# A sixth pair of gate columns by seven products, gate sigmoids at the producer, and one more LayerNorm row per half on VectorE

## The chip, the cores and the metric

The kernel runs on one core of a Trainium2 chip. The metric is the device time of one execution in microseconds (us), smaller is better; the median of several runs counts. The engines are PE (TensorE, with its weight loads listed as PEld), DVE (VectorE), ACT (ScalarE), POOL (GpSimd) and SP (SyncE, whose queue issues all the DMAs here).

## What is computed

One layer of a transformer-like trunk on x of 1024 rows and 1024 columns, all in float32:

```python
h = x @ w_in                       # 1024 x 5120: q, k, v of two head groups, gates ga, gb
y_a = chunk_band_attention(qa, ka, va, rel_bias) @ w_proj_a   # 8 softmax heads
y_b = stick_breaking_attention(qb, kb, vb) @ w_proj_b         # 8 heads, sigmoid and running products
gate_a = sigmoid(ga + b_gate[:1024]); gate_b = sigmoid(gb + b_gate[1024:])
mix = (gate_a * y_a + gate_b * y_b) @ w_out
x = layer_norm(alpha * x + mix)                               # LayerNorm 1
x = layer_norm(alpha * x + (silu(x @ wg) * (x @ wu)) @ w_ffn_out)
```

## The kernel before

Every float32 operand is split in a high and a low part (`split`, L110), and a product of two is three matmuls: high by high, high by low, low by high. Two schemes make a 1024-column projection. The plain one (`gate`, L542; `project_plain`, L314) takes 48 matmuls of 128x512 for 128 output columns. The other takes two blocks of 128 columns together as a 2 by 2 block matrix product by seven products in place of eight (`pair_steps`, L181): 7 products of 12 matmuls, 84 for 256 columns, where two plain ones take 96. It needs sums of the weights, which `prep_left`, `prep_right` and `prep_last` (L135 to L164) make on DVE and ACT.

The program runs in stages.

- **First stage** (0 to 348 us): one plain q/k pair, one plain gate (`first_gate`), seven q/k pairs by seven products, the values v (`v_stage`), and then `N_GATE` pairs of gates by seven products (`run_pairs(N_QK, len(work), ...)`). In the version before N_GATE is 5: gates 0 to 9 by seven products and gate 10 plain. Gate i = 2c + br is block c of gate a (br 0) or of gate b (br 1). A gate's columns go to DRAM (`g_dr`) without bias and sigmoid.
- **Attention** (348 to 657 us): eight softmax heads (A) and then eight stick-breaking heads (B). Per block of 128 queries PE makes scores (`sc`), ACT and DVE and POOL turn them into weights (`w`), PE transposes these (`tp`), ACT and DVE split them (`pt`), and PE multiplies by v (`pv`). In between stand filler matmuls from `fill_all` (L741): first the plain gates that are left (11 to 15 before, `gps`, 48 units each), then the projection of y_a with its gate (`yAps`, 192 units in all). Each unit is one matmul of 128x512. With the fillers come their weights' loads and splits (`load_w`, L525), the loads and splits of y_a (`split_y`, L792), the reload of a gate from DRAM with its sigmoid on ACT (`reload_gate`, L799), and a multiplication on DVE (L770).
- **y_b, output projection, LayerNorm 1** (657 to about 830 us): the same for y_b (`yBps`), the product with w_out by seven products (`ops`), and LayerNorm 1 row tile by row tile (`layer_norm`, L936), followed by transposes of the result (`x1ps`, L967).
- **FFN** (up to the end): `sxf`, `szf`, `syf` and `dn`.

How many filler units a head gets is set by FILL: the first number is the units of each A head, the second of each B head. The program adds that much to a goal over the head's steps and draws fillers up to it:

```python
        goal += FILL[hd["br"]] / nhead
        fill_until(0.5 * (last + goal))
```

Before, 8 x 16 + 8 x 38 = 432 units, which is 5 x 48 + 192. A scheduler then lays each engine's instructions in an order of its own; each engine then takes its instructions in that order.

`layer_norm` has two ways to apply the last scale and shift. The slow one, for row tiles 0, 1, 4 and 5, is one ACT pass (L951) and one POOL addition (L952) over 128x1024. The quick one, for 2, 3, 6 and 7, is two DVE instructions of 128x512 (L947).

## Time and profile before

| what | us |
|---|---|
| median of 3 runs | 1431.62 (1430.89 to 1433.25) |
| the profiled execution | 1434.07 |
| its span, first to last instruction | 1432.0 |
| granted clock of TensorE | 0.999 |
| busy PE, PEld | 1401.2, 1157.2 |
| busy DVE, ACT, POOL | 1021.5, 686.0, 309.4 |

The profile is of one execution. 2.1 us of its time lie outside the span; the median of the runs is 2.45 us below it. The end of a matmul in the records is modelled, so that matmuls overlap in them (389 ns is listed for a 128x512 matmul); how fast PE goes is read from the starts.

### The profile page before, as it was taken

Reading aid. Unit: us, or ns where it says so; the run is one execution under the profiler, and the core shown is the slowest. Engines: PE = TensorE matmul, PEld = TensorE weight load, DVE = VectorE, ACT = ScalarE, POOL = GpSimd, SP = SyncE. Lnnn points to the kernel's source line nnn. Section 1 sums busy time; section 2 is a strip of 40 time slices with the busy share of each in tenths; the row PEclk is TensorE's granted clock in tenths of the full one; section 3 lists DMA queues with packets and bytes.
Section 4 is the critical chain, followed back from the end, with each engine's and each line's share of the span. In section 5 each row is a group of like instructions: output and inputs, shape, how many; then the busy total and the mean of one; then the engine's idle time right before and its main releaser. Section 6 shows DMA issues by size and latency. Waiting matters only on the chain.

```text
span 1432.0 us, 18804 instructions
## 1 busy us (share of the span) xinstructions
PE 1401.2 (98%) x6592; PEld 1157.2 (81%) x6592; DVE 1021.5 (71%) x1588; ACT 686.0 (48%) x1196; POOL 309.4 (22%) x338
## 2 busy tenths in 40 slices
PE   8999999999999999999999999999999999999997
PEld 6888888888788787778887878888888888888886
DVE  8866467763878988986869996555556544875896
ACT  6444354544787889774223633333333332444540
POOL 0000000002444769661314021111111110200022
PEclk9999999999999999999999999999999999999999
DMA  7566737878875566747852143322332227853521
GB/s 250 169 179 182 236 89 272 304 265 253 209 211 167 173 182 206 216 161 285 317 214 81 67 160 105 106 96 108 111 105 84 91 97 258 318 193 104 170 81 74
DMA packets 98574, 248.75 MB, mean 174 GB/s; under 512 B 10400, under 2 KB 26784, under 8 KB 98480
## 3 DMA queue, kind: packets, MB, share of 16 engines
q1 hardware_dynamic: 98480, 247.56, 52.5%
q8 instruction: 52, 0.85, 0.2%
q14 instruction: 42, 0.34, 0.1%
HBM read 164.39 MB, written 83.13 MB: 173 GB/s over the span
## 4 chain that ended last, share of the span: by engine, by line
PE 84%; DVE 7%; ACT 3%; DMA 3%; issue 2%; POOL 0%; POOLq 0%; DVEq 0%; SPq 0%; ACTq 0%
PE sxf L178 15%; PE dn L1247 15%; PE sxp L178 9%; PE szf L178 7%; PE v L425 5%; PE ops L1106 5%; PE szp L178 5%; PE syf L178 4%; PE gps L549 3%; PE syp L178 2%; PE tp_b L705 2%; PE yAps L767 1%; DVE kp_b L676 1%; PE tp_a L705 1%; PE yBps L118 1%
## 5 line engine op out<-in xcount | busy, mean ns | idle before, releaser
L1247 PE MATMUL dn<-dr,dl 128*128 128x512 f32 x924 | 209.9, 389 | 0.0
L1247 PEld LDWEIGHTS dn<-dr,dl 128*128 128x128 f32 x924 | 173.4, 188 | 36.4 <-DVE x L1099 0.4
L679 POOL TENSOR_TENSOR w_b<-w_b,kp_b 128x511 f32<-128x511 f32 (+3 forms) x96 | 100.5, 1057 | 44.9 <-DVE kp_b L676 38.6
L676 DVE TENSOR_TENSOR_SCAN kp_b<-kp_b,ident_ps 128x512 f32<-128x512 f32 (+3 forms) x96 | 93.1, 970 | 18.1 <-ACT kp_b L674 14.2
L111 ACT CAST dl<-raw 128x512 fp32r<-128x512 f32 x77 | 47.2, 622 | 84.1 <-PE dn L1247 64.5
L1106 PE MATMUL ops<-wr,wl 128*128 128x512 f32 x336 | 78.8, 392 | 0.0
L943 POOL TENSOR_TENSOR mv<-mv,neghalf 128x1 f32<-128x1 f32 x16 | 26.9, 1682 | 236.3 <-DVE mv L942 236.3
L628 POOL MEMSET bias<- 64x64 f32 x8 | 1.2, 145 | 335.6 <-ACT bias L627 335.6
L1106 PEld LDWEIGHTS ops<-wr,wl 128*128 128x128 f32 x336 | 62.5, 188 | 12.5
L112 DVE TENSOR_TENSOR dl<-raw,dl 128x512 fp32r<-128x512 f32 x77 | 53.6, 703 | 25.9 <-ACT dl L111 25.7
L674 ACT ACTIVATE kp_b<-sc_b 128x512 f32<-128x512 f32 (+3 forms) x96 | 49.4, 514 | 19.7 <-PE sc_b L609 16.6
L1044 POOL TENSOR_TENSOR sb<-h 128x512 f32<-128x512 f32 x10 | 15.9, 1594 | 185.6 <-PE syf L178 135.5
L649 POOL TENSOR_SCALAR w_a<-w_a,st_a 128x640 f32<-128x640 f32 (+2 forms) x64 | 43.4, 684 | 56.7 <-DVE st_a L648 37.9
L178 PE MATMUL szf<-x1S63h,wcf 128*128 128x512 f32 x168 | 55.3, 390 | 0.0
L191 DVE TENSOR_TENSOR gt<-sxf,gt 128x512 f32<-128x512 f32 x21 | 14.4, 687 | 55.1 <-PE sxf L178 55.1
L112 DVE TENSOR_TENSOR pt_b<-tp_b,pt_b 128x512 fp32r<-128x512 f32 (+1 forms) x80 | 48.8, 621 | 6.9 <-ACT pt_b L111 6.7
L705 PE MATMUL tp_b<-ident,w_b 128*128 128x128 f32 x288 | 45.3, 274 | 5.0 <-DVE pt_b L112 3.2
L111 ACT CAST pt_b<-tp_b 128x512 fp32r<-128x512 f32 (+1 forms) x80 | 45.6, 572 | 9.1 <-PE tp_b L705 8.6
L675 ACT ACTIVATE w_b<-sc_b 128x511 f32<-128x511 f32 (+3 forms) x96 | 49.6, 517 | 0.0
L646 ACT ACTIVATE w_a<-w_a,st_a 128x640 f32<-128x640 f32 (+2 forms) x64 | 44.6, 697 | 8.8 <-DVE st_a L641 7.1
L1045 POOL TENSOR_TENSOR sa<-h,h 128x512 f32<-128x512 f32 x10 | 15.8, 1584 | 147.5 <-PE sxf L178 135.8
L112 DVE TENSOR_TENSOR pt_a<-tp_a,pt_a 128x512 fp32r<-128x512 f32 x64 | 41.6, 652 | 6.9 <-ACT pt_a L111 6.4
(1520 smaller groups left out, 4181.3 us busy)
## 6 DMA issues: line engine op xcount, KB each, us to landing
raw<-left_dr SPq DMA_DIRECT2D x77, 256.0 KB, 3.0
wo_dr<-wo SPq DMA_DIRECT2D x28, 512.0 KB, 4.0
wr<-wo_dr SPq DMA_DIRECT2D x28, 512.0 KB, 7.7
wLf<-in_w_ffn_in_dram SPq DMA_DIRECT2D x22, 512.0 KB, 4.4
wRf<-in_w_ffn_in_dram SPq DMA_DIRECT2D x22, 512.0 KB, 4.2
rows<-in_w_ffn_out_dram SPq DMA_DIRECT2D x22, 512.0 KB, 6.5
left_dr<-h SPq DMA_DIRECT2D x33, 256.0 KB, 2.0
v_dr<-vst SPq DMA_DIRECT2D x16, 512.0 KB, 3.0
```

Of the source, the lines that this page charges most:

```text
L111: nc.scalar.copy(dst_h, src)
L112: nc.vector.tensor_tensor(dst_l, src, dst_h.bitcast(F32), ALU.subtract)
L178: mm(acc, lw[:, ks], rx, start=(first and kt == i == 0), stop=(kt == 3 and i == 2), skip_group_check=not first)
L425: mm(banks[mt], xs[lw][:, ms], o[:, rx], start=(fresh and kt == n == 0), stop=(kt == 3 and n == 2), skip_group_check=not fresh)
L646: nc.scalar.activation(s[:, 0:w], s[:, 0:w], AF.Exp, bias=st[:, m:m + 1], scale=-1.0, accum_out=st[:, 2:3])
L674: nc.scalar.activation(kp[:, c0:e], sc[:, 0:n], AF.Sigmoid, scale=-1.0)
L675: nc.scalar.activation(be[:, m0:e], sc[:, m0 - c0:n], AF.Sigmoid)
L676: nc.vector.tensor_tensor_scan(kp[:, c0:e], kp[:, c0:e], ident_ps()[:, 0:n], kp[:, c0 - 1:c0] if c0 else 0.0, ALU.mult, ALU.bypass if c0 e ...
L679: nc.gpsimd.tensor_tensor(be[:, m0:e], be[:, m0:e], kp[:, m0 - 1:e - 1], ALU.mult)
L705: tr(tp[:, j:j + P], wt[qb - q0][:, (kb - qb) * P:(kb - qb + 1) * P], ident)
L1106: mm(acc, lw, rx, start=(fresh and n == m == 0), stop=(n == 3 and m == 2), skip_group_check=not fresh)
L1247: mm(acc, lw, rx, start=(fresh and steps[s][1] == n == 0), stop=(last and n == 2), skip_group_check=not fresh)
```

## The change

- N_GATE goes from 5 to 6. Gates 10 and 11 become a sixth pair by seven products at the end of the first stage, gate 12 is the plain gate early in that stage, and gates 13, 14 and 15 are the fillers that are left.
- FILL goes from (16, 38) to (12, 30): 8 x 12 + 8 x 30 = 336 units, which is 3 x 48 + 192.
- Bias and sigmoid of gates 0 to 12 are applied where the gates are made, before the store to DRAM: on the tile of 128x1024 for the paired gates, and in place of the copy out of PSUM for gate 12. `reload_gate` applies them to gates 13, 14 and 15 alone. The load of the bias moves forward.
- In LayerNorm 1, row tiles 1 and 5 take the quick way.

```diff
-FILL = (16.0, 38.0)
+FILL = (12.0, 30.0)
...
-    N_GATE = 5
+    N_GATE = 6
...
+    dma(bg, b_gate)
...
-        dma(bg, b_gate)
...
+    def gate_sigmoid(dst, src, i):
+        col = (i % 2) * 8 + i // 2
+        nc.scalar.activation(dst, src, AF.Sigmoid, bias=bg[:, col:col + 1])
...
         def out_g(side):
+            gate_sigmoid(tl[side], tl[side], 2 * pair + int(side) - 1)
             dma(g_dr[2 * pair + int(side) - 1], tl[side])
...
-            nc.scalar.copy(gt[:, cs], acc)
+            if i == 2 * N_GATE:
+                gate_sigmoid(gt[:, cs], acc, i)
+            else:
+                nc.scalar.copy(gt[:, cs], acc)
...
         dma(t, g_dr[2 * c + br])
-        col = br * 8 + c
-        nc.scalar.activation(t, t, AF.Sigmoid, bias=bg[:, col:col + 1])
+        if 2 * c + br > 2 * N_GATE:
+            gate_sigmoid(t, t, 2 * c + br)
...
-            layer_norm(acc_t[tt], g1, b1, f"1_{tt}", tt % 4 >= 2)
+            layer_norm(acc_t[tt], g1, b1, f"1_{tt}", tt % 4 >= 1)
```

After line 279 the lines of the changed program are numbered higher, by 1 at first and by 8 from the attention stage on (L646 becomes L654).

ACT's order at the seam between the first stage and attention, before. `c_12` are the two halves of the last gate pair, `wh_g` the high part of a filler gate's weights, `w_a` the first softmax blocks, to which L646 applies Exp:

```order
L208 COPY c_12_2763<-szp_2775 128x512
L366 COPY c_12_2735<-sxp_2722 128x512
L532 CAST wh_g_2944<-wr_g_2943 128x1024
L646 ACTIVATE w_a_0_0_2866,st_a_0_2867<-w_a_0_0_2866,st_a_0_2867 128x640
L646 ACTIVATE w_a_0_1_2879,st_a_1_2880<-w_a_0_1_2879,st_a_1_2880 128x640
```

The same place in the changed program, where `c_13` is the last pair:

```order
L340 ACTIVATE c_13_2906<-c_13_2906,bg 128x1024
L371 COPY c_13_2878<-sxp_2865 128x512
L537 CAST wh_g_3908<-wr_g_3907 128x1024
L340 ACTIVATE c_13_2878<-c_13_2878,bg 128x1024
L654 ACT_TABLE_LOAD
L654 ACTIVATE w_a_0_0_3001,st_a_0_3002<-w_a_0_0_3001,st_a_0_3002 128x640
```

Between the last copy out of PSUM and the first Exp there now stand a sigmoid and a load of ACT's function table, beside the cast that stood there before.

SP's queue at the same place, before. `g_dr` are the stores of the last pair's gates, `kl`, `kh`, `qs` the loads for the second head, `v` that of its values:

```order
L592 DMA kl_2855<-k_dr_85 64x1024 x2
L531 DMA wr_g_2943<-in_w_in_dram 128x1024
L360 DMA g_dr_112<-c_12_2763 128x1024
L360 DMA g_dr_111<-c_12_2735 128x1024
L601 DMA v_3006<-v_dr_93 128x8x128
L592 DMA kh_2852<-k_dr_85 64x1024
L589 DMA qs_2850<-q_dr_77 128x1024
L592 DMA kh_2852<-k_dr_85 64x1024
```

And in the changed program (`wr_y_0` are weights of the y_a projection):

```order
L365 DMA g_dr_114<-c_13_2906 128x1024
L536 DMA wr_y_0_4764<-in_w_proj_dram 128x512 x2
L365 DMA g_dr_113<-c_13_2878 128x1024
L600 DMA kl_2990<-k_dr_85 64x1024 x2
L600 DMA kh_2987<-k_dr_85 64x1024 x2
```

Both parts of the second head's keys now stand behind both gate stores; its queries stand ahead of them.

DVE's order in LayerNorm 1 around row tile 5, before (`mv_5`, `mv_6` are the statistics of row tiles 5 and 6):

```order
L944 SCALAR_TENSOR_TENSOR acc_7164<-acc_7164,mv_5_7772,ln1g 128x1024
L1097 SCALAR_TENSOR_TENSOR acc_7165<-acc_7165,ops_2_7265 128x512
L940 BN_STATS bn_6_7808<-acc_7165 128x6
L940 BN_STATS bn_7_7832<-acc_7166 128x6
L941 BN_AGGR mv_6_7809<-bn_6_7808 128x2
L942 TENSOR_SCALAR mv_6_7809<-mv_6_7809 128x1
```

And in the changed program:

```order
L952 SCALAR_TENSOR_TENSOR acc_7166<-acc_7166,mv_5_7774,ln1g 128x1024
L1105 SCALAR_TENSOR_TENSOR acc_7167<-acc_7167,ops_2_7267 128x512
L955 SCALAR_TENSOR_TENSOR acc_7166<-acc_7166,mv_5_7774,ln1b 128x512 x2
L948 BN_STATS bn_6_7810<-acc_7167 128x6
L1105 SCALAR_TENSOR_TENSOR acc_7168<-acc_7168,ops_3_7268 128x512
L949 BN_AGGR mv_6_7811<-bn_6_7810 128x2
```

The two instructions of the quick way stand right behind row tile 6's first addition. For row tile 1 they stand in the same way behind the addition of row tile 3's columns (`acc<-ops_3`).

Counted on PE between the first scores of one head and of the next, the fillers before are 16 and 4 in the first two heads, 16 in each of the next six, 20 in the head where A passes into B, then 38 each in six heads and 68 in the last with what follows it. In the changed program they are 23 and 0, then 6, 10, 12, 12, 12, 12, then 15, six times 30, and 54.

## The prediction, with the chip not yet run

> **What bounds the kernel now.** I began with the page's sums, then took the chain of work that ended last in order of time, then busy time by stretches cut at the first scores of each head (the timeline of PE gives these times), and last PE's waits.
>
> ```profile
> span 1432.0 us, 18804 instructions
> PE 1401.2 (98%) x6592; PEld 1157.2 (81%) x6592; DVE 1021.5 (71%) x1588; ACT 686.0 (48%) x1196; POOL 309.4 (22%) x338
> ```
>
> ```profile
> 181.74 71.17 PE v L425 x314
> ...
> 342.67 2.72 PE szp L178 x12
> ...
> 348.76 3.12 DMA g_dr<-c
> 352.28 8.20 DMA kh<-k_dr
> ```
>
> ```profile
> core 0: us, PE busy (x) PEld busy (x) DVE busy (x) ACT busy (x) POOL busy (x), PEclk, DMA share, GB/s
> 260.00:340.00 80.00, 80.00 (x354) 66.25 (x353) 49.55 (x69) 34.94 (x53) 0.58 (x4) 1.00 0.76 280
> 348.00:360.60 12.60, 11.17 (x62) 8.49 (x61) 9.24 (x36) 9.66 (x22) 7.62 (x9) 1.00 0.92 242
> 360.60:371.60 11.00, 10.72 (x69) 9.43 (x70) 8.54 (x35) 8.49 (x20) 4.30 (x6) 1.00 0.69 176
> 371.60:387.30 15.70, 15.26 (x96) 13.01 (x94) 12.94 (x41) 13.74 (x31) 8.39 (x16) 1.00 0.80 201
> 387.30:403.30 16.00, 15.46 (x94) 13.03 (x95) 12.75 (x43) 12.78 (x31) 8.22 (x12) 1.00 0.91 241
> 403.30:464.50 61.20, 60.99 (x378) 51.60 (x378) 50.45 (x164) 47.62 (x113) 24.27 (x40) 1.00 0.62 183
> 464.50:483.30 18.80, 17.13 (x100) 13.96 (x99) 17.50 (x28) 17.37 (x41) 13.60 (x21) 1.00 0.45 118
> 483.30:526.00 42.70, 42.70 (x246) 37.00 (x245) 36.78 (x47) 32.71 (x76) 27.96 (x43) 1.00 0.61 184
> 526.00:549.60 23.60, 21.88 (x124) 18.45 (x123) 18.53 (x24) 22.78 (x46) 20.53 (x21) 1.00 0.73 220
> 549.60:617.50 67.90, 65.30 (x368) 55.30 (x367) 61.71 (x80) 55.05 (x118) 50.43 (x69) 1.00 0.65 194
> 617.50:657.10 39.60, 36.96 (x206) 30.61 (x205) 31.81 (x44) 29.72 (x55) 17.95 (x19) 1.00 0.58 196
> 800.00:850.00 50.00, 48.03 (x212) 39.09 (x212) 49.39 (x60) 26.57 (x34) 7.37 (x4) 1.00 0.34 116
> ```
>
> The two matmul rows of the chain give PE's price: 2.72 / 12 = 71.17 / 314 = 0.2267 us for one 128x512 matmul. In 260:340 PE is busy all the time and 354 matmuls took 80 us, 0.226 each: the first stage is PE alone, with DVE at 62% and ACT at 44%. Attention is tighter. In 403:464 (four A heads) and 483:526 (two B heads with gate fillers) PE hardly stops, so there every filler costs its 0.2267 us. But DVE stands at 82% and 86% in these two, at 93% in 464:483, and at 61.71 / 67.90 = 91% in the B heads with y_a fillers, where PE idles 2.6 us. What PE waits for in 345:660 is, with one exception, an ACT, DVE or POOL result:
>
> ```profile
> PE tp_b L705 <- DVE pt_b L112: 3.2, 5, 1.8
> PE sc_b L608 <- ACT w_b L675: 2.2, 3, 1.5
> PE tp_b L705 <- POOL w_b L679: 1.7, 1, 1.7
> PE tp_a L705 <- DVE pt_a L112: 1.3, 2, 0.8
> PE sc_a L608 <- DMA kh<-k_dr: 1.2, 1, 1.2
> ```
>
> **First stage: plus 19.0 us.** The sixth pair adds 84 matmuls at the end of a stretch that is PE alone: 84 x 0.2267 = 19.04. Its splits, sums and loads come at the rate that the five pairs before it have in 260:340, so PE goes on covering them. New there are the sigmoids:
>
> ```profile
> L802 ACT ACTIVATE gA<-gA,bg 128x1024 f32<-128x1024 f32 x8 | 9.6, 1195 | 0.7 <-DVE pt_b L112 0.6 <-issue 0.2
> L770 DVE TENSOR_TENSOR gA<-yAps,gA 128x512 f32<-128x512 f32 x16 | 10.9, 679 | 0.7 <-PE yAps L767 0.5
> ```
>
> Two of 1.195 us for each pair of 19.04 us take ACT from 44% to some 56%; PE hides them, and the most they could cost, if each held PE up, is 12 x 1.2 = 14.3. I take 0, since ACT has more than half of each pair's time free. The bias load is 8 KB in SP's queue, well ahead of its use: 0. The plain gate's two sigmoids bring a function table load on ACT early in the stage; next to it PE has the following pairs' products, so 0, and at most the load's own time below.
>
> **Seam to attention: plus 1.2 us for the first two heads.** ACT's rows at the seam and at the one table load that attention has now:
>
> ```profile
> 348.15 0.59 ACT L366 COPY c<-sxp 128x512 f32<-128x512 f32 x1 [7.57 <-PE sxp L178]
> ...
> 349.80 0.83 ACT L646 ACTIVATE w_a<-w_a,st_a 128x640 f32<-128x640 f32 x1
> ...
> 465.90 1.28 ACT L674 ACT_TABLE_LOAD   x1
> 467.20 0.60 ACT L674 ACTIVATE kp_b<-sc_b 128x512 f32<-128x512 f32 x1
> ```
>
> The first Exp starts 1.65 us after the last copy out of PSUM starts. In the changed order a sigmoid (1.2) and a table load (1.28) come in between: 2.5 us later, with all the first head's weights behind it. The keys of the second head wait for the last gate's store (in the chain 3.12 us, then 8.20 us for `kh`), which the sigmoid puts off by 1.2 us, and SP holds everything behind that store. Against this PE now has 23 fillers in place of 16 before the second head's first scores, 1.6 us more work, and 0 in place of 4 in the second head. Three fillers more in these two heads are 0.7 us; the delay of 2.5 us is mostly covered by the drawn-forward work. I put the two heads at +1.2, between 0 (all covered) and +3.7 (1.2 for the store and 2.5 for Exp, nothing covered).
>
> The Trainium skill, "ScalarE: Activation LUTs", section "What ACT_TABLE_LOAD costs", gives 1.28 us for the load and another 1.38 us of drain, 2.66 for a switch. Here the first sigmoid starts 1.30 us after the load starts, so the drain does not show; with it the seam would cost some 1.4 us more by the page, an estimate.
>
> **Attention: minus 17 us of 21.8.** Ninety-six fillers leave, 96 x 0.2267 = 21.8, if PE stays the bound in every head. How much of it comes depends on DVE, whose work per head stays (scans, splits), so I go by stretch, with the fillers counted from the order, and ask what share of the new time DVE would be busy:
>
> - 371.6:403.3, 16 fillers fewer: 31.7 - 3.6 = 28.1, DVE 25.7 / 28.1 = 91%. Taken: -3.6, since PE also idles 1.0 there now.
> - 403.3:464.5, 16 fewer: 61.2 - 3.6 = 57.6, DVE 88%. Taken: -3.4.
> - 464.5:483.3, 5 fewer (1.1). DVE is at 93% with PE waiting 1.7. Taken: -0.5.
> - 483.3:526.0, 16 fewer (3.6); y_a's work starts earlier now, so one L770 of 0.68 comes in. DVE 37.5 of 39.1 would be 96%. Taken: 40.4, -2.3.
> - 526.0:549.6, 8 fewer (1.8). ACT is at 22.78 of 23.60 now; two sigmoids of 1.2 leave it, and about 2.5 L770 of 0.68 come to DVE, 20.2. At 94% that is 21.4: -2.2.
> - 549.6:617.5, 24 fewer (5.4), so two L770 fewer: DVE 60.3. PE alone would give 62.5, DVE at 96.5%. At 94%, 64.2: -3.7.
> - 617.5:657.1, 14 fewer (3.2): 36.4, DVE 85%. Taken: -2.7.
>
> Together with the first two heads: 1.2 - 3.6 - 3.4 - 0.5 - 2.3 - 2.2 - 3.7 - 2.7 = -17.2. The 94% is my choice: 93% is the most that a stretch of attention shows (464:483), 99% is shown in 800:850, where DVE's own chain is the bound and does not pass through three other engines for each block. Were the sigmoids that leave ACT (eight for a, of which one stays) the cause of PE's waits, the walls would fall below PE's price less the present idle time; that is the better end. At y_b another six sigmoids of 1.2 us leave ACT; PE idles only some tenths there, so -0.3.
>
> **LayerNorm 1: minus 0.3 us.**
>
> ```profile
> 753.58 0.69 DVE L1099 TENSOR_TENSOR acc<-ops,acc 128x512 f32<-128x512 f32 x1 [1.34 <-PE ops L1106]
> 757.60 1.41 DVE L947 SCALAR_TENSOR_TENSOR acc<-acc,mv,ln1b 128x512 f32<-128x512 f32 x2
> 778.78 1.27 DVE L944 SCALAR_TENSOR_TENSOR acc<-acc,mv,ln1g 128x1024 f32<-128x1024 f32 x1
> 782.19 2.96 DVE L944 SCALAR_TENSOR_TENSOR acc<-acc,mv,ln1g 128x1024 f32<-128x1024 f32 x1
> ```
>
> ```profile
> 781.72 2.35 POOL L952 TENSOR_TENSOR acc<-acc,ln1b 128x1024 f32<-128x1024 f32 x1 [1.26 <-ACT acc L951]
> ```
>
> ```profile
> PE sxf L178 <- DVE gt L191: 2.0, 2, 1.7
> PE x1ps L967 <- POOL acc L952: 1.8, 1, 1.8
> ```
>
> The quick way costs DVE 1.41 us a row tile. For tile 1 the two instructions fall into the 1.34 us in which DVE waits for PE: 0.1. For tile 5 they come ahead of tile 6's statistics, but the POOL addition goes, and with it the stretch of tile 6's L944, which took 2.96 beside that addition and 1.27 without: 1.41 - 1.69 = -0.3. PE's wait of 1.8 us for that addition goes too, but DVE is 99% busy in 800:850 and PE waits for it there again (2.0 us), so what PE gains at 784 it waits at 847. Hence -0.3, between -1.8 (the wait gained whole) and +1.4 (one tile's instructions wholly late).
>
> **Sum.** 19.04 - 17.2 - 0.3 - 0.3 = +1.2 us on the profiled 1434.07, 1435.3. The median of the runs is 2.45 below that execution, so 1432.8 is what I predict for the median, no change within 0.2% (2.9 us), which is about what a measurement of this kernel can tell.
>
> **Rivals.**
>
> *Faster: PE stays the bound.* For it: 403:464 and 483:526 are PE's alone, and ACT loses 8.4 us of sigmoids in attention, so that waits such as the 1.7 in 526:549 may vanish. Then attention gives 21.8 and 1.7 more, less 1.2 at the seam: -22.3. With 19.04 and LayerNorm's and y_b's -0.6 that is -3.9: 1427.8. Against it: DVE would have to be 96% busy over 68 us, and the one A-to-B stretch at 93% has PE waiting. Chance 0.28.
>
> *Slower: DVE's queue takes PE's place in B.* From 483 on every B head but the first carries y_a fillers in the change, so the stretch that is 91% DVE grows from three heads to some four and a half. If DVE cannot go above that 91%, the walls are 37.5 / 0.91 = 41.2, 20.2 / 0.91 = 22.2 and 60.3 / 0.91 = 66.3: -1.5, -1.4 and -1.6 in place of -8.2. The sum rises by 3.7, and by a further 1 if 617:657 keeps its share: +5.9, 1437.5. The point from which it decides is DVE's share in 549:617: at 93% the result is still within 0.2%, at 91% it is slower. Chance 0.22.
>
> *Slower: the seam.* Nothing covered, +3.7 in place of 1.2, gives 1435.3 on top of the forecast's other terms. Chance 0.07.
>
> *The fillers were free.* If PE has room in attention, removing them saves nothing there and the change costs 19 - 0.6: 1450. Busy PE is no proof against it, since the ends of matmuls are modelled; the evidence is that the starts follow each other at the 0.2267 of the first stage and that 483:526 shows no idle. Chance 0.03.
>
> **How the numbers follow.** The forecast itself, within 2.9 us of 1431.62, has 0.40. Faster by over 0.2% is the first rival, with a little of the forecast's lower edge: 0.29 and 0.39 left for no change. Slower is the three others: 0.32. The range for 8 in 10 goes from 1427.2, the first rival with half a microsecond more, to 1438.6, the DVE rival with 1.1 more for part of the seam.
>
> **What would show it.** In the changed profile the last gate pair should end 19.0 us later, at 367; the first `w_a` Exp some 4 us after that; the B heads with y_a fillers should show DVE at 93 to 95%; L944 of tile 6 should take 1.3; attention should last about 292 us from the first scores to the first `yBps` in place of 309. The prediction is wrong if attention lasts under 288 (PE was the bound) or over 296 (DVE was), or if PE waits in the first stage.

## The result, and the profile after

The changed kernel takes 1440.80 us (median of six runs, 1439.77 to 1442.36) where the kernel before, on the same chip, takes 1432.09 (median of five runs, 1430.89 to 1433.64; a sixth was in a slow state, at 1973.62, and is left out). The ratio is 1.0060 with a 95% interval of 1.0046 to 1.0074: slower by some 8.6 us, more than the 0.2% that a measurement can tell, and above the upper end of the predicted range. The profiled execution took 1442.36.

The page's first lines of the changed kernel:

```profile
span 1440.6 us, 18799 instructions
PE 1404.1 (97%) x6580; PEld 1157.6 (80%) x6580; DVE 1033.1 (72%) x1603; ACT 688.0 (48%) x1197; POOL 303.1 (21%) x334
```

Twelve matmuls fewer, yet PE's busy time grew by 2.9 us: some of its matmuls were slower. Where the 8.6 us of span come from is read by stage, cut at the first scores (348.0 before, 368.6 after), the first `yBps` (657.1, 668.0), the first `ops` (701.7, 712.8) and the first `sxf` (798.4, 806.8):

| stage | before | after | difference | predicted |
|---|---|---|---|---|
| up to the first scores | 348.0 | 368.6 | +20.6 | +19.0 |
| attention | 309.1 | 299.4 | -9.7 | -17.2 |
| y_b | 44.6 | 44.8 | +0.2 | -0.3 |
| output projection and LayerNorm 1 | 96.7 | 94.0 | -2.7 | -0.3 |
| FFN and the rest | 633.6 | 633.8 | +0.2 | 0 |

Attention is the stage that failed. Its stretches in the changed kernel, cut at the first scores of a head as in the prediction (heads are counted from 0; 0 to 7 are A, 8 to 15 are B); the rows from 518.60 on are heads 10, 11, 12, then 13 with 14, and 15:

```profile
core 0: us, PE busy (x) PEld busy (x) DVE busy (x) ACT busy (x) POOL busy (x), PEclk, DMA share, GB/s
368.60:392.00 23.40, 23.04 (x134) 18.49 (x132) 17.38 (x68) 20.12 (x43) 10.90 (x15) 1.00 0.73 202
392.00:419.40 27.40, 27.17 (x172) 23.27 (x173) 24.74 (x85) 23.80 (x59) 12.64 (x23) 1.00 0.70 196
419.40:479.80 60.40, 58.40 (x362) 48.84 (x361) 51.11 (x166) 45.79 (x109) 24.21 (x40) 1.00 0.66 189
479.80:498.10 18.30, 16.16 (x95) 12.81 (x94) 17.01 (x26) 16.95 (x41) 12.91 (x23) 1.00 0.53 146
498.10:518.60 20.50, 19.84 (x116) 16.98 (x115) 18.54 (x25) 17.42 (x40) 14.54 (x22) 1.00 0.75 230
518.60:541.40 22.80, 20.01 (x115) 16.81 (x114) 20.26 (x26) 19.90 (x43) 22.80 (x25) 1.00 0.66 186
541.40:565.60 24.20, 21.43 (x116) 18.25 (x115) 21.61 (x24) 15.52 (x34) 16.30 (x23) 0.93 0.59 196
565.60:591.70 26.10, 21.56 (x115) 18.09 (x114) 21.78 (x28) 17.34 (x40) 16.67 (x24) 0.93 0.48 141
591.70:632.10 40.40, 39.85 (x230) 33.82 (x230) 38.69 (x52) 32.95 (x75) 27.03 (x42) 1.00 0.63 196
632.10:668.00 35.90, 33.85 (x191) 27.79 (x190) 31.08 (x42) 26.61 (x52) 15.79 (x19) 1.00 0.53 183
```

Heads 9, 13 and 14 take 20.1 to 20.5 us each; heads 10, 11 and 12, with the same work on PE, take 22.8, 24.2 and 26.1, together 12 us more. DVE is not their bound: it is at 96% in 591.7:632.1, where PE hardly stops, and below 90% in the three slow heads, where its busy time even holds waits for POOL, as shown below. Two things stand out. POOL is busy for the whole of 518.6:541.4. And the granted clock is 0.93 over 541.4:591.7, 1.00 in every other row.

PE's waits in attention (line numbers are 8 higher than before):

```profile
PE tp_b L713 <- DVE pt_b L112: 11.5, 8, 2.8
PE sc_b L616 <- ACT w_b L683: 2.2, 2, 1.8
PE tp_a L713 <- DVE pt_a L112: 1.7, 3, 0.8
```

The wait for `pt_b` was 3.2 before. Four waits make most of the two sums, by the timeline of PE (the wait stands in brackets, it ends at the row's start):

```profile
526.47 0.66 PE L713 MATMUL tp_b<-ident,w_b 128*128 128x128 f32 x4 [2.79 <-DVE pt_b L112]
549.29 1.11 PE L713 MATMUL tp_b<-ident,w_b 128*128 128x128 f32 x4 [2.77 <-DVE pt_b L112]
567.98 0.50 PE L616 MATMUL sc_b<-kh,qs 128*128 128x512 f32 x1 [1.77 <-ACT w_b L683]
575.48 0.66 PE L713 MATMUL tp_b<-ident,w_b 128*128 128x128 f32 x4 [2.77 <-DVE pt_b L112]
```

Each of the three on DVE lies at the start of a head. There DVE adds the two halves of the last head's values (`yt`, L741, 64x1024, both operands in SBUF; 1.22 to 1.32 us in eleven of the fourteen), then does two scans, then the subtractions for which PE waits. DVE before the first of these waits:

```profile
520.75 2.57 DVE L741 TENSOR_TENSOR yt<-yt 64x1024 f32<-64x1024 f32 x1
523.24 2.59 DVE L684 TENSOR_TENSOR_SCAN kp_b<-kp_b,ident_ps 128x512 f32<-128x512 f32 x2
525.75 1.26 DVE L112 TENSOR_TENSOR pt_b<-tp_b,pt_b 128x512 fp32r<-128x512 f32 x2
```

and POOL at the same time, where `yl` is a filler's subtraction (`split_y`):

```profile
519.84 2.39 POOL L805 TENSOR_TENSOR yl<-yraw,yh 128x1024 fp32r<-128x1024 f32 x1
522.20 1.44 POOL L687 TENSOR_TENSOR w_b<-w_b,kp_b 128x127 f32<-128x127 f32 x1
523.60 2.35 POOL L805 TENSOR_TENSOR yl<-yraw,yh 128x1024 fp32r<-128x1024 f32 x1
```

The addition takes 2.57 us in place of 1.22. POOL's subtraction ends at 522.23, the addition at 523.32, 1.09 later: it does nearly its whole work after POOL's instruction. POOL's next one, a 128x127 multiplication that takes 0.46 elsewhere, takes 1.44 and ends 0.32 after the addition: now POOL waited. At the start of head 11 DVE loses three times running (the second POOL row below holds two multiplications):

```profile
542.03 3.98 DVE L741 TENSOR_TENSOR yt<-yv_b 64x1024 f32<-64x1024 f32 x1
```

```profile
541.43 2.40 POOL L538 TENSOR_TENSOR wl_y<-wr_y,wh_y 128x1024 fp32r<-128x1024 f32 x1
543.78 1.15 POOL L687 TENSOR_TENSOR w_b<-w_b,kp_b 128x255 f32<-128x255 f32 x2
```

Again it ends 1.08 us after the last of the POOL instructions, 544.93. The wait of 1.77 on ACT has another path to the same engine: ACT's cast of a filler weight waits in ACT's queue for a POOL subtraction to free its buffer, and the sigmoids of `w_b` stand behind it:

```profile
566.54 1.04 ACT L537 CAST wh_y<-wr_y 128x1024 fp32r<-128x1024 f32 x1 [2.22 <-POOL yl L805]
```

After two of the three waits of 2.8 us the granted clock fell to one half. Three microseconds after each of them, in order 549.29, 575.48 and 526.47:

```profile
549.50:552.50 3.00, 3.00 (x10) 2.42 (x10) 2.89 (x4) 0.59 (x1) 1.67 (x3) 0.50 0.43 157
...
576.80:579.80 3.00, 3.00 (x11) 2.41 (x10) 2.50 (x4) 0.59 (x1) 2.36 (x4) 0.50 0.73 202
...
526.50:529.50 3.00, 3.00 (x18) 2.56 (x19) 2.89 (x4) 1.18 (x2) 3.00 (x3) 1.00 1.01 229
```

Ten and eleven matmuls start where eighteen did. A clock of 0.93 over 24.2 and 26.1 us is 1.7 and 1.8 us lost, 3.5 in all.

At the other two ends: PE's new wait in the first stage, with ACT's rows beside it,

```profile
PE sxp L178 <- ACT gate L340: 1.1, 1, 1.1
```

```profile
45.37 1.28 ACT L340 ACT_TABLE_LOAD   x1
46.67 0.69 ACT L340 ACTIVATE gate<-gps,bg 128x512 f32<-128x512 f32 x1
```

and its waits from 700 to 1222, where the 1.8 us on POOL in LayerNorm 1 went and did not come back at `sxf`:

```profile
PE sxf L178 <- DVE gt L191: 1.8, 2, 1.4
PE x1ps L975 <- DVE acc L955: 0.2, 1, 0.2
```

### The profile page after: what moved, and what is told of

Its sections match the earlier page's. It is cut to its first block, busy times and chain, and to the rows that moved or that the text cites. A ratio compares the mean times of both kernels' runs of the same rounds, so it can differ in the third digit from the quotient of the medians.

```text
span 1440.6 us, 18799 instructions
## 1 busy us (share of the span) xinstructions
PE 1404.1 (97%) x6580; PEld 1157.6 (80%) x6580; DVE 1033.1 (72%) x1603; ACT 688.0 (48%) x1197; POOL 303.1 (21%) x334
## 4 chain that ended last, share of the span: by engine, by line
PE 85%; DVE 8%; ACT 2%; issue 2%; DMA 1%; POOL 1%; SPq 0%; POOLq 0%; DVEq 0%; ACTq 0%
PE sxf L178 15%; PE dn L1255 15%; PE sxp L178 10%; PE szf L178 8%; PE v L430 5%; PE ops L1114 5%; PE szp L178 5%; PE syf L178 4%; PE yAps L775 2%; PE syp L178 2%; PE tp_b L713 2%; PE tp_a L713 1%; PE gps L554 1%; DVE kp_b L684 1%; PE sc_a L616 1%
## 5 line engine op out<-in xcount | busy, mean ns | idle before, releaser
L1114 PEld LDWEIGHTS ops<-wr,wl 128*128 128x128 f32 x336 | 62.5, 188 | 12.5
L112 DVE TENSOR_TENSOR dl<-raw,dl 128x512 fp32r<-128x512 f32 x77 | 53.5, 701 | 24.2 <-ACT dl L111 24.1
L1052 POOL TENSOR_TENSOR sb<-h 128x512 f32<-128x512 f32 x10 | 20.3, 2027 | 184.4 <-PE syf L178 134.1
L713 PE MATMUL tp_b<-ident,w_b 128*128 128x128 f32 x288 | 46.5, 280 | 11.6 <-DVE pt_b L112 11.5
L713 PEld LDWEIGHTS tp_b<-ident,w_b 128*128 128x128 f32 x288 | 35.5, 143 | 22.1 <-DVE pt_b L112 14.0
L654 ACT ACTIVATE w_a<-w_a,st_a 128x640 f32<-128x640 f32 (+2 forms) x64 | 44.5, 696 | 4.9 <-DVE st_a L649 4.0
```

The lines of the kernel that those rows point to most:

```text
L112: nc.vector.tensor_tensor(dst_l, src, dst_h.bitcast(F32), ALU.subtract)
L654: nc.scalar.activation(s[:, 0:w], s[:, 0:w], AF.Exp, bias=st[:, m:m + 1], scale=-1.0, accum_out=st[:, 2:3])
L713: tr(tp[:, j:j + P], wt[qb - q0][:, (kb - qb) * P:(kb - qb + 1) * P], ident)
L1114: mm(acc, lw, rx, start=(fresh and n == m == 0), stop=(n == 3 and m == 2), skip_group_check=not fresh)
```

## The experiments

Eighteen kernels, in five groups; each group shares one chip and the runs of the kernel before on it. "Ratio" is the time against these, with its 95% interval.

| run | median, us | before there | ratio |
|---|---|---|---|
| the change | 1440.80 | 1432.09 | 1.0060 (1.0046 to 1.0074) |
| ln_only | 1430.57 | 1434.17 | 0.9979 (0.9970 to 0.9989) |
| sig_only | 1438.97 | 1434.17 | 1.0033 (1.0022 to 1.0045) |
| pair_only | 1439.62 | 1434.17 | 1.0033 (1.0020 to 1.0047) |
| add_by_half | 1445.82 | 1434.17 | 1.0083 (1.0068 to 1.0098) |
| split_dve | 1437.20 | 1433.61 | 1.0032 (1.0020 to 1.0043) |
| dma_splits | 1431.03 | 1433.61 | 0.9979 (0.9970 to 0.9987) |
| plain_copy | 1440.63 | 1433.61 | 1.0046 (1.0032 to 1.0061) |
| ln_split_dve | 1434.64 | 1433.61 | 1.0008 (0.9999 to 1.0016) |
| pool_single | 1432.44 | 1433.47 | 0.9991 (0.9982 to 1.0000) |
| ln_dma | 1430.67 | 1433.47 | 0.9982 (0.9973 to 0.9991) |
| mixed | 1438.98 | 1433.47 | 1.0037 (1.0024 to 1.0050) |
| pair_ln_mixed | 1435.61 | 1433.47 | 1.0013 (1.0004 to 1.0021) |
| pieces4 | 1443.44 | 1433.93 | 1.0067 (1.0055 to 1.0079) |
| pieces2 | 1440.68 | 1433.93 | 1.0048 (1.0036 to 1.0060) |
| ln_pieces4 | 1434.76 | 1433.93 | 1.0005 (0.9997 to 1.0014) |
| pair_ln_pieces4 | 1439.74 | 1433.93 | 1.0038 (1.0025 to 1.0051) |
| free_y4 | 1433.48 | 1434.68 | 0.9994 (0.9985 to 1.0002) |
| free_late | 1433.04 | 1434.68 | 0.9986 (0.9976 to 0.9995) |

**The three parts alone.** On the kernel before, LayerNorm 1 only:

```diff
-            layer_norm(acc_t[tt], g1, b1, f"1_{tt}", tt % 4 >= 2)
+            layer_norm(acc_t[tt], g1, b1, f"1_{tt}", tt % 4 >= 1)
```

> Before with the LayerNorm edit alone (row tiles 1 and 5 the quick way). The prediction's term was -0.3 us, because VectorE was taken to hand back what PE gains. The changed profile reads otherwise: from the first output-projection matmul to the first dn matmul it takes 510.0 us against 512.2. If the edit is the whole of that, this kernel is 2 us faster than before; if the prediction's term holds, no difference can be measured.

the sigmoids only (N_GATE 5 and FILL as before),

```diff
+            gate_sigmoid(tl[side], tl[side], 2 * pair + int(side) - 1)
             dma(g_dr[2 * pair + int(side) - 1], tl[side])
...
+            if i == 2 * N_GATE:
+                gate_sigmoid(gt[:, cs], acc, i)
...
+        if 2 * c + br > 2 * N_GATE:
+            gate_sigmoid(t, t, 2 * c + br)
```

> Before with bias and sigmoid at the producers alone (five gate pairs, fillers 16 and 38, LayerNorm as before). Theory A, the sigmoids leave ACT where it is full (526:549) and cost little elsewhere: 2 us faster or so, since the 1.7 us wait there goes and some tenths at y_b. Theory B, the two table loads and the sigmoid in front of Exp take it back: the 1.1 us wait of PE for the plain gate's sigmoid appears at about 47 us, the seam costs one more us, and the sum is within 1 us of before or slower.

and the sixth pair only, the sigmoids where they were:

```diff
-FILL = (16.0, 38.0)
+FILL = (12.0, 30.0)
...
-    N_GATE = 5
+    N_GATE = 6
```

> Before with the sixth pair and fillers 12 and 30 alone (sigmoid at the reload, LayerNorm as before). If the loss of the whole change (8.7 us) comes from the fillers taken out of attention, this kernel is slower than before by 8.7 plus the 2 us that LayerNorm gave, less the 1.3 us of the table load at the start: some 9 us, 1441. If moving the sigmoids is what hurts, it is slower by less than 5.

LayerNorm 1 gains 0.21% (3.0 us); the other two cost 0.33% (4.7 us) each. The parts add up to 0.45%, the whole is 0.60%, within the intervals. In sig_only theory B had the sign, and its 1.1 us wait at the start came; but 3.6 us of the loss lie in the B heads (196.2 us in place of 192.6), which neither theory had. pair_only, slower by 4.7 us by the ratio and 5.5 by the medians, stands at the border of its two cases and decides nothing between them. Both parts that cost do it in the same way. In pair_only the additions at the starts of heads 10, 11 and 12 take 2.57, 1.99 and 3.03 us, and PE waits 2.79, 1.64 and 3.02 there. In sig_only head 12 takes 28.0 us in place of 22.6, PE's longest wait of attention is 4.04 us at 560.85, and ahead of it stands this addition:

```profile
552.79 4.43 DVE L741 TENSOR_TENSOR yt<-yt 64x1024 f32<-64x1024 f32 x1
```

```profile
551.64 1.73 POOL L687 TENSOR_TENSOR w_b<-w_b,kp_b 128x383 f32<-128x383 f32 x2
553.31 2.41 POOL L538 TENSOR_TENSOR wl_y<-wr_y,wh_y 128x1024 fp32r<-128x1024 f32 x1
555.67 0.47 POOL L687 TENSOR_TENSOR w_b<-w_b,kp_b 128x127 f32<-128x127 f32 x1
```

With the sigmoids moved, the scheduler laid this weight's subtraction two places further up in POOL's order, ahead of the 128x127 multiplication and the one behind it, so that the addition met it. The addition ends at 557.22, 1.08 after POOL's last.

**The addition in halves.** After the change, every head's addition in two instructions of 64x512, as the last head has it:

```diff
-                    if hd["i"] == 7:
+                    if True:
```

> The changed kernel with the addition of the value halves (64x1024, both operands in SBUF, which took 2.6 to 4.0 us on VectorE beside a POOL split at three head starts, where PE then waits 2.8 us) made in two parts of 64x512, one behind each half of the head, as the last pair of heads has it already. VectorE's sum of work stays. Theory A, the loss in B is that one long instruction in front of the scans at the head's start: the three waits of 2.8 us fall by half or more, 4 to 6 us faster than the changed kernel, so 3 to 5 us slower than before. Theory B, VectorE's share of the time is the bound: no difference from the changed kernel, 8.7 us slower than before.

Slower still, 1.0083. The waits for `pt_b` got shorter (2.24 at most), but others on ACT's `w_b` of 2.1 and 2.5 us came, and head 10 had POOL at 100% over 24.8 us. Neither theory had that. A half takes 0.69 us alone, and three of them took 2.11, 2.04 and 1.65 beside POOL: now each of two additions per head can be held. That the length of this one addition is the cause fell with it.

**Where POOL's subtractions go.** The subtractions of the fillers' y tiles and projection weights, 11 in all, from POOL to VectorE (the four places like this; the two of the plain gates' weights stay on POOL):

```diff
-                        split_y((28, 34, 40, 46).index(n), nc.gpsimd)
+                        split_y((28, 34, 40, 46).index(n), nc.vector)
```

> The whole change, with the subtractions that belong to the fillers in attention (the plain gates' and the projections' weights, and the y tiles: some 13 of 128x1024, 2.4 us each on GpSimd) on VectorE. Theory 'GpSimd is full and slows VectorE': PE's waits in heads 8 to 12 of attention, 12.9 us in the changed kernel against 5.1 in the kernel before, fall to about 6, the added 13 x 1.24 us of VectorE lie beside PE's work, and the time is 1433 to 1436. Rival 'VectorE's share of time is the limit, as predicted': 16 us more on VectorE lengthen attention by 5 to 10 us, to 1446 to 1451.

all 13 subtractions of the fillers taken away; a DMA copies the high part into the low part's place, so the kernel leaves the low parts out, and PE's work is the same:

```diff
-        lo_eng.tensor_tensor(lo, r, hi.bitcast(F32), ALU.subtract)
+        if lo_eng is nc.gpsimd:
+            dma(lo.bitcast(F32), hi.bitcast(F32))
...
-        eng.tensor_tensor(yl[i], raw, yh[i].bitcast(F32), ALU.subtract)
+        dma(yl[i].bitcast(F32), yh[i].bitcast(F32))
```

> The whole change, with those same subtractions left out and the second operand filled by a copy that a DMA makes of the first, so that it costs neither GpSimd nor VectorE anything (the low parts of these operands are left out of the arithmetic; PE's work is the same). Theory 'GpSimd is full and slows VectorE': the value addition of VectorE takes 1.4 to 1.9 us at the start of each head instead of up to 4, GpSimd stays under 80% in head 10, PE's waits in heads 8 to 12 fall from 12.9 to under 6 us and the time to 1431 to 1435. Rival 'VectorE's own chain at the start of a head, too long for the fewer fillers': the waits stay over 10 us and the time within 2 us of 1440.8.

the plain gate's sigmoid back at its reload:

```diff
-            if i == 2 * N_GATE:
-                gate_sigmoid(gt[:, cs], acc, i)
-            else:
-                nc.scalar.copy(gt[:, cs], acc)
+            nc.scalar.copy(gt[:, cs], acc)
...
-        if 2 * c + br > 2 * N_GATE:
+        if 2 * c + br >= 2 * N_GATE:
```

> The whole change, but the one plain gate at the start of the program is copied as before and takes its sigmoid where it is read again. Theory 'the table load in front of that sigmoid is paid in full': first scores 1.2 to 1.6 us earlier, 1439.3 to 1439.8, with the waits of attention as they are. Rival 'that load is hidden, or comes back at the next sigmoid': 1440.8 plus or minus 0.4.

and the kernel before with LayerNorm 1 as changed and the subtractions on VectorE:

> The kernel before, with the part of the change in LayerNorm 1 alone (1430.6 when run by itself) and the fillers' subtractions on VectorE. Theory 'GpSimd is full and slows VectorE': PE's waits in heads 8, 11 and 13 of attention (1.7, 1.7 and 1.8 us) shrink too and the time is 1427 to 1429.5. Rival 'VectorE's share is the limit': 1434 to 1438.

dma_splits is the run that decides: 1431.03, 9.8 us under the changed kernel by the medians (on two chips; by the ratios, each against the kernel before on its own chip, 0.81%, some 11.6 us). Heads 10, 11 and 12 there:

```profile
517.40:539.30 21.90, 20.16 (x115) 16.97 (x114) 19.32 (x25) 18.93 (x42) 12.61 (x21) 1.00 0.82 244
539.30:559.40 20.10, 20.01 (x115) 16.92 (x115) 19.13 (x26) 16.41 (x37) 12.48 (x21) 1.00 0.81 259
559.40:579.70 20.30, 19.79 (x115) 16.98 (x115) 19.64 (x27) 17.35 (x38) 12.48 (x21) 1.00 0.87 266
```

```profile
PE tp_b L716 <- DVE pt_b L112: 4.2, 8, 0.8
```

Heads 11 and 12 are at the 20 us of their neighbours (22.8, 24.2 and 26.1 became 21.9, 20.1 and 20.3; 1.2 us of the first is a wait for the copy itself), every addition of these heads takes 1.22, the clock is 1.00. The order is not the cause: in these three heads PE's 341 matmuls and DVE's 76 instructions of the changed kernel stand in the same order in dma_splits, ACT's nearly so (110 of 115), and POOL's are the same but for the seven subtractions and one multiplication at the edge. DVE stands at 95% and 97% in the last two rows with PE idle for 0.1 and 0.5 us, so DVE's share is not what bounded these heads. VectorE instead of POOL (split_dve) gets only 3.6 us back: head 10 then is VectorE's,

```profile
516.80:540.50 23.70, 20.57 (x116) 16.77 (x115) 23.56 (x29) 20.27 (x44) 15.96 (x20) 1.00 0.62 179
```

99% busy over 23.7 us. Neither theory's number came there (1433 to 1436, or 1446 to 1451): both engines have too little room in that one head. In ln_split_dve, on the longer heads of the kernel before, the move costs: 1434.64 (ratio 1.0008), in the rival's range, against 1430.57 (0.9979) for LayerNorm 1 alone on another chip.

In plain_copy the first scores start at 366.4 in place of 368.6, but 1.0 of these 2.2 us is there before the sigmoid can play a part: the plain gate's first matmul starts at 30.85 in place of 31.88 (32.83 in ln_only, so this start varies by itself). Counted from it, the first scores come after 335.5 us in place of 336.7: the table load and the sigmoid at the plain gate cost 1.2 us at that point. The 1440.63 lies in the rival's range. The time of the whole is lower by 0.14% by the ratios, but the intervals overlap, and the profiled execution was 2.3 us longer between the first `sxf` and the first `dn`, where nothing was changed (418.3 us there, 416.0 in the changed kernel); whether it pays in the end stays open.

**What in the subtractions does it.** Two one-input operations of POOL in place of each subtraction, nearly as long together, each half as long (the low parts are left out here too):

```diff
+            for _ in range(2):
+                lo_eng.tensor_scalar(lo, hi.bitcast(F32), 1.0, 0.0, ALU.mult, ALU.add)
```

> The whole change, with each of the fillers' subtractions on GpSimd replaced by two one-input operations of GpSimd on the same tile (each some 1.1 us by the 0.684 us of a 128x640 one, so that GpSimd is taken for nearly as long as by one subtraction of 2.4; the low parts are left out of the arithmetic, PE's work is the same). Theory 'sharing': a two-input operation of GpSimd slows VectorE's two-input operations beside it. Then VectorE's value addition takes 1.4 to 1.9 us at the head starts, not up to 4.0, PE's waits in heads 8 to 12 fall from 12.9 to under 8 us, and the time to 1433 to 1436, though GpSimd stays near full in head 10. Rival 'queue': the subtractions stand in front of the w_b multiplications in GpSimd's queue and hold them. Then the waits stay over 10 us and the time is 1438.5 to 1441.

the kernel before with LayerNorm 1 as changed and the DMA's copies (again without the low parts), for the price of the pair without the subtractions:

> The kernel before with LayerNorm 1 as changed, and the fillers' subtractions replaced by a DMA's copy as in the whole change at 1431.0 (low parts left out; PE's work the same as in the kernel before). It says whether the sixth pair with its sigmoids pays once GpSimd's subtractions cost nothing. Theory 'the trade is even at best, +20 us before attention and at most -20 in it': 1427 to 1430 here, so the pair still costs 1 to 4 us. Rival 'only the subtractions stood against the pair': 1431 or more here, so the pair would be level or gain.

the subtractions divided between the engines,

```diff
-                        split_y((28, 34, 40, 46).index(n), nc.gpsimd)
+                        split_y((28, 34, 40, 46).index(n), (nc.vector, nc.gpsimd)[n % 4 // 2])
...
-            nxt = load_proj(0, cc + 1, "op", nc.gpsimd) if cc < 3 else None
+            nxt = load_proj(0, cc + 1, "op", nc.vector) if cc < 3 else None
```

> The whole change, with the first and third of the four y subtractions and those of the projections' later weights on VectorE, the rest on GpSimd. Theory 'GpSimd and VectorE both stand near full in heads 10 to 12, so that the best is a division': 1434 to 1436.5, under the 1437.2 of all on VectorE and the 1440.8 of all on GpSimd, with the granted clock of attention's second half back at 1.00. Rival 'any two-input work of GpSimd beside the head starts costs as much as it saves': 1437 to 1440.

and this without the sigmoids at the producers (the two edits of mixed on pair_only with LayerNorm 1 as changed):

> As the one before, but without the sigmoids at the producers: the sixth pair, LayerNorm 1, and the subtractions divided between VectorE and GpSimd. Theory 'the sigmoids at the producers cost 1.2 to 1.4 us at the start (a table load and a sigmoid in front of the first products) and return nothing, since ScalarE is no bound in attention': 1 to 3 us under the one before, 1431.5 to 1434.5. Rival 'ScalarE's sigmoids at the reload cost about as much in attention': the same within 1 us.

pool_single takes 1432.44: 8.4 of the 9.8 us are back, a little more than 'sharing' had said, though POOL does nearly as much in head 10:

```profile
517.50:539.10 21.60, 20.04 (x115) 16.81 (x115) 19.03 (x26) 19.95 (x43) 21.41 (x29) 1.00 0.64 180
```

But its traces correct the theory as I had put it. A one-input operation of POOL holds the addition too:

```profile
561.38 1.64 DVE L745 TENSOR_TENSOR yt<-yt 64x1024 f32<-64x1024 f32 x1
```

```profile
560.87 1.07 POOL L540 TENSOR_SCALAR wl_y<-wh_y 128x1024 fp32r<-128x1024 f32 x1
561.90 1.43 POOL L691 TENSOR_TENSOR w_b<-w_b,kp_b 128x127 f32<-128x127 f32 x1
```

561.94, the end of POOL's, plus 1.08 is again the addition's end. It is not slowed, it waits for its turn, and a shorter instruction makes that turn shorter. ln_dma and dma_splits are level (0.9982 and 0.9979): without these subtractions the sixth pair with its sigmoids costs and gains the same. The 1430.67 lies between the ranges of its theory and its rival. ln_dma is level with ln_only too (0.9979), so in the kernel before the same subtractions cost nothing that shows. That holds with a reserve, since the copies brought ln_dma new waits on `w_b`, and a stretch at 0.57 of the clock in head 13. Dividing helps less than hoped, mixed is at 1438.98 (1437.20 with all on VectorE), within its rival's range. pair_ln_mixed, without the sigmoids at the producers, is 3.4 us under mixed, and over its range; by the two traces 1.2 of that is there at the first scores (367.6 against 368.8), 0.6 comes in the A heads and 1.8 in the B heads.

**Shorter instructions.** Each subtraction of POOL in four, and in two, with the same arithmetic:

```diff
-        eng.tensor_tensor(yl[i], raw, yh[i].bitcast(F32), ALU.subtract)
+        for c in range(0, 1024, 256):
+            cs = slice(c, c + 256)
+            eng.tensor_tensor(yl[i][:, cs], raw[:, cs], yh[i][:, cs].bitcast(F32), ALU.subtract)
```

> The whole change, with each of the fillers' subtractions on GpSimd cut into four instructions of 256 columns (some 0.65 us each; the arithmetic is the same). Theory 'VectorE's addition waits until the GpSimd instruction under way ends': the additions at the head starts take 1.3 to 2.3 us in place of 2.6 to 4.0, PE's waits in heads 8 to 12 fall from 12.9 to some 7 us, no half clock, 1433 to 1436. Rival 'two inputs on GpSimd slow the addition whatever their length, or GpSimd's fullness holds w_b': additions over 2.5 us still, 1439 to 1442.

> As the one before with two instructions of 512 columns (some 1.25 us each). Theory 'waits out the instruction under way': additions of 1.3 to 2.9 us, between the two: 1434 to 1438, and at or over the one in four pieces. Rival 'two inputs or fullness': 1439 to 1442.

> The kernel before with LayerNorm 1 as changed (1430.6 by itself) and the subtractions in four pieces. Theory 'waits out the instruction under way': the two additions that took 1.88 and 2.51 us there take 1.3 to 1.9, and the time is 1429 to 1430.6; since taking the subtractions away altogether gave 1430.7 there, no more than that can come. Rival 'the pieces' own overhead counts': 1431 to 1433.

> Sixth pair and LayerNorm 1 without the sigmoids at the producers, the subtractions in four pieces. Theory 'the sixth pair is level once the subtractions don't hold VectorE': 1430 to 1433. Rival 'GpSimd is full in head 10 all the same and holds w_b': 1434 to 1438.

All four missed the theory's numbers: 1443.44 (over its rival's too) and 1440.68, no better than the change; the two others 1434.76 and 1439.74, over their rivals' too. Of the additions of pieces4, two of three did get short, 1.32 and 1.61 us in place of 2.57 and 2.56, and each still ends 1.08 after a POOL instruction. In pieces2 they took 1.60 and 1.47, but the third, at the start of head 11, took 4.16: it waited out four POOL instructions in a row, so shorter ones need not mean a shorter wait. But the pieces take longer together (4 x 0.779 = 3.1 us for one of 2.39), and head 10 paid for it:

```profile
L810 POOL TENSOR_TENSOR yl<-yraw,yh 128x256 fp32r<-128x256 f32 x28 | 20.8, 779 | 0.4 <-ACT yh L807 0.4
```

```profile
519.30:545.80 26.50, 21.93 (x115) 18.18 (x114) 19.12 (x26) 20.07 (x43) 26.50 (x41) 0.94 0.56 162
```

Its wall is POOL's busy time (POOL's own waits for DVE count as busy), 26.5 us; POOL was full over the whole head at 22.8 in the changed kernel and 23.6 in pieces2 too. In the changed kernel PE's one long wait in that head is the 2.79 us for DVE. In pieces4 and pieces2 it waited there for POOL's own `w_b` as well, for the first and the second time below:

```profile
PE tp_b L716 <- POOL w_b L690: 2.3, 1, 2.3
PE tp_b L716 <- POOL w_b L690: 1.6, 1, 1.6
```

So two things of POOL's cost time: whole instructions that DVE must wait out, and a head that is full of POOL's work. Cutting trades the one for the other.

**Which subtractions.** The four y subtractions that fall into head 10 replaced by a DMA's copy, the others on POOL (`if i < 4` in `split_y`), and the other way round (the projections' weights and the later y tiles replaced); what is replaced leaves out its low parts:

> The whole change, with only the four y subtractions that fall into head 10 replaced by a DMA's copy (their low parts left out). Theory 'head 10 is GpSimd's': its wall falls from 22.8 to about 21 us with GpSimd at some 70%, heads 11 and 12 keep their waits, and 1 to 3 us come back: 1438 to 1440. Rival 'the full queue of head 10 is what puts the later subtractions beside the head starts': heads 11 and 12 fall too, 1431 to 1435.

> The whole change, with the other group replaced by a DMA's copy: the projections' weights and the later y tiles; the four y subtractions of head 10 stay. Theory 'heads 11 and 12 lose by single held instructions': head 10 stays at 22 to 23 us, heads 11 and 12 fall from 24.2 and 26.1 to 20 to 21, no half clock, and 6 to 9 us come back: 1432 to 1435. Rival 'what head 10 piles up is carried into heads 11 and 12': less than 4 us, 1437 or more.

1433.48 and 1433.04: either group gives 7 to 8 us of the 9.8 back, so their prices don't add. Without the four, head 10 falls from 22.8 to 20.5 us, and heads 11 and 12 fall with it, to 21.1 and 21.4: what 'rival' had said of that run. Without the others, head 10 stays (24.3 us, a half clock in it) and heads 11 and 12 fall to 20.1 and 20.6: what 'theory' had said of that one. So the long waits of heads 11 and 12 seem to need both: the delay that head 10 hands on, and a long subtraction in the way. In free_y4 a subtraction still holds the addition at the start of head 11, for 2.22 us, and PE waits only 1.09 there. How the delay is handed on was not followed through the traces.

No kernel with the sixth pair that computes the whole reference beats the kernel before. Of the kernels that compute it, only ln_only does, at 0.9979.

## Why the prediction was wrong, step by step

**The step that failed** is "attention: minus 17 us of 21.8", in its B heads, and in it the question that was put to each stretch: "what share of the new time DVE would be busy". The stretches of the prediction, with what they gained in the changed kernel and in dma_splits:

| heads | predicted | the change | subtractions by DMA |
|---|---|---|---|
| 0, 1 | +1.2 | -0.2 | -1.0 |
| 2, 3 | -3.6 | -4.3 | -3.4 |
| 4 to 7 | -3.4 | -0.8 | -1.6 |
| 8 | -0.5 | -0.5 | -0.5 |
| 9, 10 | -2.3 | +0.6 | -0.3 |
| 11 | -2.2 | +0.6 | -3.5 |
| 12 to 14 | -3.7 | -1.4 | -6.8 |
| 15 | -2.7 | -3.7 | -3.7 |
| sum | -17.2 | -9.7 | -20.8 |

The 94% of DVE bounded nothing: in heads 11 and 12 of dma_splits DVE is at 95 and 97% with PE idle for 0.1 and 0.5 us. What lengthened heads 10 to 12 was POOL's subtractions: they take 73.1 us with them and 62.3 without. The forecast counted fillers as matmuls only and put their subtractions at nothing, without a reason. Their price comes in two ways. The larger part is that DVE's additions wait out whole POOL instructions and PE waits behind them: pool_single, with POOL still busy for 21.41 of 21.6 us in head 10 but in shorter instructions, got 8.4 us back. The other part is a full POOL, and the row for it stood in the prediction, unread: POOL was busy 20.53 of 23.60 us in 526:549.6, with four y subtractions, and in the change these fall into head 10, for which the forecast had some 20.2 us (half of 40.4). Their place counts too: before, the first of them started 5.6 us behind the start of its head and none met an addition; in the change the first starts at 516.77, 1.8 us ahead of the start of head 10, and the next one holds the addition there. A head that gets shorter keeps POOL's work, 12.5 us of `w_b` (dma_splits shows it alone), and in this one head four y subtractions of 2.39 and one weight of 2.42 on top.

**The DVE rival** (1437.5) had the right sign and place, B heads from 483 on, but its mechanism is refuted by the same rows. **PE stays the bound** (1427.8) is nearly what dma_splits shows in attention, -20.8 against -22.3, once POOL's subtractions are gone. That the fillers were free is refuted: attention got 9.7 us shorter even so. The seam was no loss: the first Exp starts 4.1 us after the first scores in place of 1.9, much as forecast, and heads 0 and 1 still gained 0.2.

**The A heads** came out right in sum (-5.3 for -5.8) by luck, since the parts were wrong: in heads 4 to 7 sixteen fillers fewer gave 0.8 us and not 3.4, in dma_splits 1.6, so a filler there was worth 0.05 to 0.1 us and not 0.2267. Busy PE without recorded waits was no proof that each of its matmuls has its full price: 60.99 of 61.2 us were busy before, and 58.40 of 60.40 after.

**First stage**: 84 x 0.2267 was the right size, and 0 was right for the pairs' sigmoids: from the plain gate's first matmul to the first scores plain_copy, which has them, takes 19.0 us more than the kernel before (335.5 and 316.5). "The plain gate's two sigmoids ... 0, and at most the load's own time" was not: PE waited 1.1 us there, the first scores came 1.6 us later than forecast, and 1.2 us, counted from the plain gate, went with the sigmoid in plain_copy. The cover I named, the products behind it, was not there, since PE's next product needs a bank that the plain gate holds until its sigmoid has read it; that last reason is argued from the wait's name and not tested.

**LayerNorm 1**: predicted -0.3, between -1.8 and +1.4; the stage shows -2.7 and ln_only 3.0 (1.6 to 4.3 by the interval). The step "what PE gains at 784 it waits at 847" failed: the wait for `gt` stayed at 1.8 (2.0 before). The wait for `x1ps` fell by 1.6; where the other 1.1 us of the stage came from is open. The stretch of tile 6's L944 went as forecast.

## What to carry to other kernels

When a stretch gets shorter, put each engine's unchanged work in it against the new length, also that of the engine with the lowest share over the whole kernel: POOL, at 21%, was full in one head of sixteen, and its long instructions held VectorE and then PE at the starts of three. Where a chain has a VectorE operation with two SBUF operands, look for long GpSimd instructions beside it: it waits out whole ones. A wait of 2 to 3 us on PE can cost a further 1.7 us in granted clock.

## What the runs showed of the hardware

- VectorE's addition of two SBUF operands (64x1024) takes 1.22 us alone. Beside POOL it ended 1.07 to 1.09 us after the end of the POOL instruction that held it, in each of the cases looked at (2.51 us before; 2.57, 3.98 and 2.56 after; 1.32 to 2.85 in pieces4; 1.47 to 4.16 in pieces2; 1.35 to 1.66 in pool_single), with one or two inputs on POOL. A scan, with one operand in PSUM, kept its time (1.21 us for the first of the two at 523.24, while POOL's next subtraction ran). The Trainium skill, "SBUF — State Buffer", section "SBUF: two separate sides", says that a VectorE operation with two SBUF inputs and a GpSimd operation that reads SBUF take a shared pair of ports in turn, each for its whole instruction. The trace agrees: the addition did 1.07 to 1.09 of its 1.22 us after the other's end. Why DVE lost three turns running at 542.03, four in pieces2 and only one at 520.75 is open.
- PE's clock went to one half for some 3.4 us (1.7 us lost) after two of three waits of 2.8 us. In ln_dma it did so after shorter waits, none over 1.03 us, in 4 us of which PE was busy for 2.1:

```profile
574.00:578.00 4.00, 2.12 (x8) 0.88 (x7) 3.13 (x4) 4.00 (x10) 1.77 (x2) 1.00 1.01 376
578.00:582.00 4.00, 4.00 (x15) 3.31 (x16) 3.89 (x5) 1.39 (x3) 2.95 (x4) 0.57 1.01 248
```

  The Trainium skill, "TensorE: Matmul & The Clock Gate", section "What's actually happening", has the clock halved after an idle window of about 3.4 us that runs freely, until a busy one. The length of the slow stretches agrees; that a full idle window is needed does not, since PE idled less than 3.4 us here each time.
- A POOL subtraction of 128x1024 took 2.39 us in one, 2 x 1.36 = 2.7 in two and 4 x 0.78 = 3.1 in four instructions; on VectorE 1.19 to 1.22 in five of seven cases of split_dve.
